# One operation per product term, and transposes planned with an advance, in a two-layer decoder trunk

## The chip, the cores and the metric

The kernel runs on one core of a Trainium2 chip. The metric is the time of one execution in microseconds (us), as the median of several runs. The engines of the core work side by side, each through its own queue in order: TensorE (matrix products and transposes, PE in the profile), VectorE (DVE), ScalarE (ACT), GpSimd (POOL) and SyncE (SP), which issues the transfers from memory.

## The reference, cut to what matters

256 tokens of width 1024 pass two layers. Each has a mixer (block-sparse attention with 16 heads in layer 0, dilated attention with 12 heads in layer 1) and a squared-ReLU MLP of width 4096, each followed by a layer norm.

```python
def reference(x, moba_w_qkv, moba_w_o, dil_w_qkv, dil_w_o, mlp_w_in, mlp_w_out, ...):
    h = x
    for i in range(DEPTH):
        ...
        h = layer_norm(DEEPNORM_ALPHA * h + mix, ln_mix_g[i], ln_mix_b[i])
        h = layer_norm(DEEPNORM_ALPHA * h + sq_relu_mlp(h, mlp_w_in[i], mlp_w_out[i]),
                       ln_mlp_g[i], ln_mlp_b[i])
    return h
```

With 256 tokens the block-sparse attention has one block, so it is plain causal attention.

## The kernel before

**Split products.** Each float32 operand is split into a high part (rounded to the matrix engine's float32r) and a low part (the rest). A product is the sum of three terms: high by high, high by low and low by high. For a weight tile, `load_w` (line 323) loads 128x1024 numbers into `raw`, ScalarE rounds them into `whi` (line 309) and VectorE subtracts to get `wlo` (line 314). `raw` has 4 buffers, `whi` and `wlo` 10 each (`NSLOT`). For the activations, `xs[0]` and `xs[1]` hold the transposed input of the current layer, each for four of the eight k tiles (128 rows of the width), with the high and the low part side by side.

**Kinds of product.** `mm_wstat` (line 440) keeps a weight tile stationary and moves all 256 tokens: it serves the query and key projections. `mm_xstat` (line 466) keeps 128 tokens of `xs` stationary and moves weight columns. It serves the values of both layers and the first chunk of each MLP, for one half of the tokens at a time (`m` is 0 or 1). In both, one recorded operation holds the three terms of one k tile, and needs the high and low part of both operands. `mm_wstat_wide` (line 453) serves the other MLP chunks. `mm_rows` (line 481) makes the output projections. All sums of one accumulation go to one PSUM buffer, so each recorded product depends on the one before it there.

**The planner.** Nothing is issued at once. Each step is recorded with `op` (line 100): its engine, an estimated cost, what it reads and writes. `Plan.order` (line 131) then fixes the order of every engine's queue. A first pass walks the operations in recorded order and gives each TensorE operation a due time, its start in that pass. A backward pass gives every other operation the latest time at which it must start for what follows, and lowers a due time where a successor needs it. Then the plan is simulated: on each engine, among the operations that can start earliest, the one with the lowest due time is taken (VectorE may wait a little for a more urgent one). Loads keep their recorded order. At run time every engine works through its queue in the planned order, whatever the real durations are.

**Stages.** Layer 0's query, key and value projections, scores, softmax and weighting follow `ORDER0`: `qk` is a pair of projections with the rotation (`rotate`, line 511: three products on VectorE, lines 514 to 519, which show as L501, a sum on GpSimd, L503, then splits), `v` the values (`do_v`), `s` the scores and the softmax, `o` the weighting, whose transposed weights ScalarE copies out as `pt` (L595). Then `out_and_ln` (line 722) does the output projection and the layer norm. The last `ntail` input tiles (from `TAIL`, one entry for each of the four sub-layers) are done half by half, the others for both halves at once. The entry for layer 1's mixer is `TAIL[2]`, which has six tiles in all.

**Junctions.** In `out_and_ln` the first half's products come first, then its `ln_half` (line 668), then the second half's products, then `between()`, then the second half's `ln_half`. `between` is the head of the next sub-layer, which works on the first half alone: for the MLPs the first chunk's `half(0)` (line 771) with `relu_sq_tok` (ScalarE lines 749 and 750 into `hrt`, then transposes), after layer 0's MLP the values of layer 1 (`layer1_head`). `ln_half` ends with two groups of four transposes (`transposes`, line 582, shown as L587) of the normed tokens `tok`, and a split into `xs`. The last sub-layer has no `between`.

Of the kernel before, what the change touches and what calls it, by code (L numbers as in the profile page):

```python
# [26 lines left out]
BIG = 3.0e38  # L27
NCH = DFF // 512
NX = (1, 1)
TAIL = (5, 5, 5, 8)  # L30
NSLOT = 10
ADD_ENG = "POOL"
ORDER0 = (
# [43 lines left out]


class Op:
    __slots__ = ("n", "eng", "cost", "fn", "preds", "succs", "bufs", "due", "wait", "ready", "end", "xfer", "early")  # L80


class Plan:
# [13 lines left out]
        self.first.setdefault(tag, b)  # L97
        return b

    def op(self, eng, cost, fn, reads=(), writes=(), xfer=0.0, early=0.0):  # L100
        o = Op()
        o.n, o.eng, o.cost, o.fn, o.xfer = len(self.ops), eng, cost, fn, xfer
        o.early = early
        o.preds, o.succs, o.bufs = set(), [], set()
        for group, is_write in ((reads, False), (writes, True)):
            for item in group:
                b, key = item if isinstance(item, tuple) else (item, None)
                o.bufs.add(b)
                for k, st in b.state.items():
                    if key is None or k is None or k == key:  # L110
                        if st[0] is not None:
                            o.preds.add(st[0])
                        if is_write:
                            o.preds.update(st[1])
                st = b.state.setdefault(key, [None, []])
                if is_write:
                    if key is None:
                        b.state = {None: [o, []]}
                    else:
                        st[0], st[1] = o, []  # L120
                else:
                    st[1].append(o)
        o.preds.discard(o)
        for p in o.preds:
            p.succs.append(o)
        for b in o.bufs:
            b.left += 1
        self.ops.append(o)
        return o

    def order(self):
        clock = {e: BEGIN[e] for e in ("PE", "SP")}
        bus = 0.0
        for o in self.ops:
            t = max([clock.get(o.eng, 0.0)] + [p.end + latency(p, o) for p in o.preds])
            o.end = t + o.cost
            if o.eng in clock:
                clock[o.eng] = o.end
            if o.xfer:
                bus = o.end = max(t + FETCH, bus) + o.xfer  # L140
            o.due = t if o.eng == "PE" else None
        t = clock["PE"]
        for o in reversed(self.ops):
            for q in o.succs:
# [104 lines left out]
def tile_trunk(  # L249
# [188 lines left out]
        return [(xs[kt // 4], (part, kt, m)) for part in range(2) for m in ms]  # L438

    def mm_wstat(ps, w):  # L440
        for kt in range(KT):

            def go(kt=kt):
                c = slice(kt * P, (kt + 1) * P)
                a, b = (xs[kt // 4].t[:, kt % 4, part, :] for part in range(2))
                first, last = kt == 0, kt == KT - 1
                mm(ps.t[:, :S], w.hi.t[:, c], a, first, False)
                mm(ps.t[:, :S], w.hi.t[:, c], b, False, False)
                mm(ps.t[:, :S], w.lo.t[:, c], a, False, last)

            op("PE", 0.36, go, [(w.hi, 0), (w.lo, 0)] + xk(kt, (0, 1)), [ps])

    def mm_wstat_wide(ps, w):
        def go_hi(kt):
# [8 lines left out]
        for kt in range(KT):  # L463
            op("PE", 0.12, lambda kt=kt: go_lo(kt), [(w.lo, 0)] + xk(kt, (0, 1)), [ps])

    def mm_xstat(ps, ws, m, n):
        t = slice(m * P, (m + 1) * P)
        for kt in range(KT):
            per = 1024 // n
            w = ws[kt // per]  # L470

            def go(kt=kt, w=w):
                c = slice((kt % per) * n, (kt % per + 1) * n)
                a, b = (xs[kt // 4].t[:, kt % 4, part, t] for part in range(2))
                mm(ps.t[:, :n], a, w.hi.t[:, c], kt == 0, False)
                mm(ps.t[:, :n], a, w.lo.t[:, c], False, False)
                mm(ps.t[:, :n], b, w.hi.t[:, c], False, kt == KT - 1)

            op("PE", 3 * (n / 2400 + 0.0135), go, [(w.hi, 0), (w.lo, 0)] + xk(kt, (m,)), [ps])

    def mm_rows(pieces, item, m):
        (ahi, alo, j), w, pos, total = item
# [99 lines left out]
    def transposes(ps, pairs, r):  # L582
        ident = late["ident"]

        def go():
            for c, src in pairs:
                nc.tensor.transpose(ps.t[:, c : c + P], src(), ident.t)  # L587

        op("PE", 0.109 * len(pairs), go, list(r) + [ident], [ps])

    halves = (slice(0, P), slice(P, S))

# [72 lines left out]
    def act_tiles():  # L665
        return mk([P, 4, S], F32R, "ahi", 3), mk([P, 4, S], F32R, "alo", 3)

    def ln_half(pieces, m, gb, last):
        g, b = gb
        z = xtok[m]  # L670
        step = min(n for _, _, n in pieces)
# [18 lines left out]
        for n in range(2):  # L690
# [12 lines left out]
            if not last:  # L703
                ps = psum("tp")
                transposes(
                    ps, [(j * P, lambda k=n * 4 + j: z.t[:, k * P : (k + 1) * P]) for j in range(4)], [(z, n)]
                )
                t = slice(m * P, (m + 1) * P)
                keys = [(n * 4 + j, m) for j in range(4)]
# [12 lines left out]
    def out_and_ln(acc, items, ntail, gb, last, between):  # L722
# [4 lines left out]
        for m in range(2):  # L727
# [2 lines left out]
                    mm_rows([piece], item, m)  # L730
            if m == 1 and between:
                between()
            ln_half(acc[m], m, gb, last)

    def relu_sq_T(ps, ahi, alo, j):
        u = mk([P, S], F32, "ta", 5)
# [23 lines left out]
    class Mlp:  # L760
# [10 lines left out]
        def half(self, m):  # L771
            ps = [psum("tp") for _ in range(self.nx)]
            for c in range(self.nx):
                mm_xstat(ps[c], self.ws[c], m, 512)
            for c in range(self.nx):
                relu_sq_tok(ps[c], m, *self.chunks[c])

# [38 lines left out]
    def layer0(between):  # L816
# [3 lines left out]
        def do_v(n):  # L820
# [4 lines left out]
            V[n] = []  # L825
            for m in range(2):
                ps = psum("tp" if n == m == 0 else "acc")
                mm_xstat(ps, ws, m, 512)
                V[n].append(evac_v(ps, 512))

        def softmax(q, k):
# [63 lines left out]
    def v1(i, m):  # L895
# [191 lines left out]
```

## Time and profile before

| | us |
|---|---|
| median of 3 runs | 579.99 (579.93 to 580.3) |
| the profiled execution | 579.34 |
| its span, first to last instruction | 577.2 |
| TensorE busy | 562.7 |
| VectorE busy | 431.3 |
| ScalarE busy | 299.9 |
| GpSimd busy | 36.9 |

A row of the timeline has the start and the duration in us, the engine, the line of the code, the operation, output and inputs by the program's names, shapes, and a count. In brackets stands how long the engine was idle just before and which engine and line ended that. PE is TensorE with matrix products, PEld its loading of the stationary operand, which runs beside. A matrix product is pipelined, so its modelled duration (0.39 us for 512 columns) is longer than the distance to the next one. Helpers record most operations, so line 318 stands for every matrix product, 309 for every rounding on ScalarE and 314 for every subtraction on VectorE.

### The profile page before, as it was taken

The numbers are of one execution on the slowest core, as the hardware profiler recorded it, in microseconds if no ns is written. First come the engines' busy times: TensorE is split into PE (matmuls) and PEld (weight loads), VectorE is DVE, ScalarE is ACT, GpSimd is POOL, SyncE is SP. The second block draws the span as 40 slices with busy tenths as digits, with TensorE's granted clock in tenths as the row PEclk, the third lists the DMA queues.
The fourth block names the chain that finished last, engine by engine and source line by source line (L and its number), as shares of the span: only waits on it lengthen the run. The fifth ranks groups of instructions, "written<-read, shape, count | busy, mean of one in ns | idle before, by whom it ended". The sixth has DMA issues, their size and how long they took to land.

```text
span 577.2 us, 8665 instructions
## 1 busy us (share of the span) xinstructions
PE 562.7 (97%) x3234; PEld 486.2 (84%) x3234; DVE 431.3 (75%) x771; ACT 299.9 (52%) x501; POOL 36.9 (6%) x41
## 2 busy tenths in 40 slices
PE   9899999999999999999999999999999999999994
PEld 8789887778888888888887998877888888888884
DVE  6899888998875675675678699988976756756544
ACT  6585666747554555454534445744754544544400
POOL 0210131010000000000000222000000000000000
PEclk9999999999999999999999999999999999999998
DMA  8646843728877666565525424544888655655101
GB/s 322 219 148 188 292 140 99 223 83 276 274 248 279 204 196 190 178 213 184 182 75 177 186 75 127 168 148 161 281 279 258 202 185 178 204 183 183 36 1 73
DMA packets 30281, 105.61 MB, mean 183 GB/s; under 512 B 3488, under 2 KB 4256, under 8 KB 30240
## 3 DMA queue, kind: packets, MB, share of 16 engines
q1 hardware_dynamic: 30240, 105.07, 55.6%
q8 instruction: 25, 0.41, 0.3%
q14 instruction: 16, 0.13, 0.1%
HBM read 104.01 MB, written 1.05 MB: 182 GB/s over the span
## 4 chain that ended last, share of the span: by engine, by line
PE 89%; DVE 7%; ACT 2%; issue 2%; POOL 1%; DVEq 0%; POOLq 0%
PE acc L318 50%; PE tp L318 37%; PE tp L587 2%; DVE wlo L314 2%; DVE ta L501 2%; DVE tok L508 1%; POOL ta L503 1%; ACT sc L573 1%; DVE klo L508 0%; DVE sc L580 0%; DVE xs L314 0%; DVE bst L682 0%; ACT hrt L749 0%; DVE qlo L314 0%; ACT hrt L750 0%
## 5 line engine op out<-in xcount | busy, mean ns | idle before, releaser
L314 DVE TENSOR_TENSOR wlo<-raw,whi 128x1024 fp32r<-128x1024 f32 (+2 forms) x185 | 225.7, 1226 | 88.1 <-ACT whi L309 86.7
L309 ACT ACTIVATE whi<-raw 128x1024 fp32r<-128x1024 f32 (+2 forms) x184 | 191.1, 1047 | 144.3 <-PE tp L318 64.9
L318 PE MATMUL acc<-whi,ahi 128*128 128x512 f32 (+1 forms) x312 | 119.5, 383 | 0.0
L318 PE MATMUL acc<-wlo,ahi 128*128 128x512 f32 (+1 forms) x312 | 117.5, 380 | 0.0
L318 PE MATMUL tp<-xs,whi 128*128 128x512 f32 x448 | 112.0, 392 | 0.0
L318 PE MATMUL acc<-whi,alo 128*128 128x512 f32 (+1 forms) x312 | 100.5, 380 | 0.0
L318 PEld LDWEIGHTS tp<-xs,whi 128*128 128x128 f32 x448 | 81.2, 189 | 14.7
L318 PE MATMUL acc<-xs,whi 128*128 128x256 f32 x448 | 83.6, 289 | 0.0
L318 PEld LDWEIGHTS acc<-xs,whi 128*128 128x128 f32 x448 | 70.4, 194 | 2.5 <-issue 1.6
L318 PEld LDWEIGHTS acc<-whi,ahi 128*128 128x128 f32 x312 | 58.8, 188 | 11.3 <-issue 0.9
L318 PEld LDWEIGHTS acc<-wlo,ahi 128*128 128x128 f32 x312 | 58.8, 188 | 10.4
L318 PEld LDWEIGHTS acc<-whi,alo 128*128 128x128 f32 x312 | 57.1, 189 | 10.4
L318 PEld LDWEIGHTS tp<-xs,wlo 128*128 128x128 f32 x448 | 61.0, 191 | 4.2
L318 PE MATMUL tp<-xs,wlo 128*128 128x256 f32 x448 | 62.7, 283 | 0.0
L318 PE MATMUL acc<-xs,wlo 128*128 128x256 f32 x224 | 62.1, 284 | 0.0
L318 PEld LDWEIGHTS acc<-xs,wlo 128*128 128x128 f32 x224 | 42.8, 192 | 0.0
L501 DVE TENSOR_TENSOR ta<-acc,ropet 64x256 f32<-64x256 f32 (+1 forms) x84 | 35.1, 421 | 9.7 <-PE acc L318 8.6
L309 ACT ACTIVATE ahi<-ta 128x256 fp32r<-128x256 f32 x56 | 22.9, 409 | 28.5 <-DVE ta L508 28.5
L503 POOL TENSOR_TENSOR ta<-ta,ta 128x256 f32<-128x256 f32 x28 | 28.2, 1014 | 119.8 <-DVE ta L501 105.8
L688 POOL TENSOR_TENSOR rstd<-rstd,expo 128x1 f32<-128x1 f32 x8 | 7.9, 987 | 414.6 <-DVE rstd L686 414.6
L318 PE MATMUL acc<-whi,xs 128*128 128x512 f32 (+1 forms) x112 | 32.9, 364 | 0.9 <-DVE xs L314 0.6
L501 DVE TENSOR_TENSOR ta<-tp,ta 128x256 f32<-128x256 f32 x56 | 23.5, 419 | 7.9 <-ACT ta L739 7.9
(83 smaller groups left out, 548.2 us busy)
## 6 DMA issues: line engine op xcount, KB each, us to landing
raw<-in_win_dram SPq DMA_DIRECT2D x64, 512.0 KB, 4.3
raw<-in_wout_dram SPq DMA_DIRECT2D x64, 512.0 KB, 4.2
raw<-in_wqk_dram SPq DMA_DIRECT2D x24, 512.0 KB, 4.0
raw<-in_wo_dram SPq DMA_DIRECT2D x14, 512.0 KB, 3.3
raw<-in_wv_dram SPq DMA_DIRECT2D x8, 512.0 KB, 6.1
g<-in_lng_dram SPq DMA_DIRECT2D x4, 512.0 KB, 7.0
b<-in_lnb_dram SPq DMA_DIRECT2D x4, 512.0 KB, 8.0
raw<-in_wv1a_dram SPq DMA_DIRECT2D x4, 512.0 KB, 3.2
```

The lines of the kernel that those rows point to most:

```text
L309: op("ACT", act(n, sbuf=sbuf), lambda: nc.scalar.activation(hi(), src(), AF.Copy), r, whi)
L314: lambda: nc.vector.tensor_tensor(lo(), src(), f32(hi()), op=ALU.subtract), list(r) + list(whi), wlo,
L318: nc.tensor.matmul(out_ap, lhsT, rhs, start=start, stop=stop)
L501: op("DVE", dve(n) + extra, lambda: nc.vector.tensor_tensor(out_ap(), a(), b(), op=alu), r, w)
L503: op("POOL", n / 480 + 0.17, lambda: nc.gpsimd.tensor_tensor(out_ap(), a(), b(), op=alu), r, w)
L508: lambda: nc.vector.scalar_tensor_tensor(dst(), a(), s(), b(), op0=o0, op1=o1), r, w,
L573: lambda: nc.scalar.activation(e(), e(), AF.Exp, bias=bias(), scale=-1.0, accum_out=total()), r, w,
L587: nc.tensor.transpose(ps.t[:, c : c + P], src(), ident.t)
L688: op("POOL", 0.98, lambda: nc.gpsimd.tensor_tensor(rs.t[:, 1:2], rs.t[:, 0:1], expo.t, op=ALU.pow), [(rs, 0), expo], [(rs, 1)])
```

## The change

`mm_wstat` records two operations for each k tile: first all high parts of the weights (two terms each), then all low parts. `mm_xstat` does the same and takes a word that says which operand lands late: for the MLP heads and layer 1's values it is `x`, so the terms with the high part of `xs` come first and the low part of `xs` last; for layer 0's values it is `w`, so the low part of the weights comes last. Operations depend only on the parts that they read. The number of matrix products and their shapes stay.

Operations can be recorded with `ahead`, which is taken off the due time. The transposes of the second half's layer norm have 1.5 us of it where there is a `between`. `TAIL[2]` goes from 5 to 6, so that all six tiles of layer 1's output projection are done half by half.

```diff
-TAIL = (5, 5, 5, 8)
+TAIL = (5, 5, 6, 8)
...
-    def op(self, eng, cost, fn, reads=(), writes=(), xfer=0.0, early=0.0):
+    def op(self, eng, cost, fn, reads=(), writes=(), xfer=0.0, early=0.0, ahead=0.0):
...
-        o.early = early
+        o.early, o.ahead = early, ahead
...
-            o.due = t if o.eng == "PE" else None
+            o.due = t - o.ahead if o.eng == "PE" else None
...
     def mm_wstat(ps, w):
+        def go_hi(kt):
+            for part in range(2):
+                mm(ps.t[:, :S], w.hi.t[:, kt * P : (kt + 1) * P], xs[kt // 4].t[:, kt % 4, part, :], kt + part == 0, False)
+
+        def go_lo(kt):
+            mm(ps.t[:, :S], w.lo.t[:, kt * P : (kt + 1) * P], xs[kt // 4].t[:, kt % 4, 0, :], False, kt == KT - 1)
+
         for kt in range(KT):
-
-            def go(kt=kt):
-                c = slice(kt * P, (kt + 1) * P)
-                a, b = (xs[kt // 4].t[:, kt % 4, part, :] for part in range(2))
-                first, last = kt == 0, kt == KT - 1
-                mm(ps.t[:, :S], w.hi.t[:, c], a, first, False)
-                mm(ps.t[:, :S], w.hi.t[:, c], b, False, False)
-                mm(ps.t[:, :S], w.lo.t[:, c], a, False, last)
-
-            op("PE", 0.36, go, [(w.hi, 0), (w.lo, 0)] + xk(kt, (0, 1)), [ps])
+            op("PE", 0.24, lambda kt=kt: go_hi(kt), [(w.hi, 0)] + xk(kt, (0, 1)), [ps])
+        for kt in range(KT):
+            op("PE", 0.12, lambda kt=kt: go_lo(kt), [(w.lo, 0)] + xk(kt, (0, 1)), [ps])
...
-    def mm_xstat(ps, ws, m, n):
+    def mm_xstat(ps, ws, m, n, late):
+
         t = slice(m * P, (m + 1) * P)
-        for kt in range(KT):
-            per = 1024 // n
+        per = 1024 // n
+
+        def go(kt, terms, first, last):
             w = ws[kt // per]
-
-            def go(kt=kt, w=w):
-                c = slice((kt % per) * n, (kt % per + 1) * n)
-                a, b = (xs[kt // 4].t[:, kt % 4, part, t] for part in range(2))
-                mm(ps.t[:, :n], a, w.hi.t[:, c], kt == 0, False)
-                mm(ps.t[:, :n], a, w.lo.t[:, c], False, False)
-                mm(ps.t[:, :n], b, w.hi.t[:, c], False, kt == KT - 1)
-
-            op("PE", 3 * (n / 2400 + 0.0135), go, [(w.hi, 0), (w.lo, 0)] + xk(kt, (m,)), [ps])
+            c = slice((kt % per) * n, (kt % per + 1) * n)
+            for i, (x_part, w_part) in enumerate(terms):
+                mm(
+                    ps.t[:, :n], xs[kt // 4].t[:, kt % 4, x_part, t], (w.hi, w.lo)[w_part].t[:, c],
+                    first and kt + i == 0, last and kt == KT - 1,
+                )
+
+        third = (1, 0) if late == "x" else (0, 1)
+        for terms, first, last in ((((0, 0), third[::-1]), True, False), ((third,), False, True)):
+            for kt in range(KT):
+                w = ws[kt // per]
+                op(
+                    "PE", len(terms) * (n / 2400 + 0.0135),
+                    lambda kt=kt, terms=terms, first=first, last=last: go(kt, terms, first, last),
+                    [((w.hi, w.lo)[i], 0) for i in {t[1] for t in terms}]
+                    + [(xs[kt // 4], (i, kt, m)) for i in {t[0] for t in terms}],
+                    [ps],
+                )
...
-        op("PE", 0.109 * len(pairs), go, list(r) + [ident], [ps])
+        op("PE", 0.109 * len(pairs), go, list(r) + [ident], [ps], ahead=ahead)
...
-            ln_half(acc[m], m, gb, last)
+            ln_half(acc[m], m, gb, last, 1.5 if m == 1 and between else 0.0)
...
-                mm_xstat(ps[c], self.ws[c], m, 512)
+                mm_xstat(ps[c], self.ws[c], m, 512, "x")
...
-                mm_xstat(ps, ws, m, 512)
+                mm_xstat(ps, ws, m, 512, "w")
...
-        mm_xstat(ps, wv[i], m, v_cols[i])
+        mm_xstat(ps, wv[i], m, v_cols[i], "x")
```

More of the change, by code (lines that the diff above doesn't have):

```diff
@@ L79 @@
 class Op:
-    __slots__ = ("n", "eng", "cost", "fn", "preds", "succs", "bufs", "due", "wait", "ready", "end", "xfer", "early")
+    __slots__ = ("n", "eng", "cost", "fn", "preds", "succs", "bufs", "due", "wait", "ready", "end", "xfer", "early", "ahead")
 class Plan:
@@ L580, in scale_by, with transposes @@
         op("DVE", dve(n, 1, True), lambda: nc.vector.tensor_scalar(e(), e(), s(), None, op0=ALU.mult), r, w)
-    def transposes(ps, pairs, r):
+    def transposes(ps, pairs, r, ahead=0.0):
         ident = late["ident"]
@@ L666, in act_tiles, with ln_half @@
         return mk([P, 4, S], F32R, "ahi", 3), mk([P, 4, S], F32R, "alo", 3)
-    def ln_half(pieces, m, gb, last):
+    def ln_half(pieces, m, gb, last, ahead):
         g, b = gb
@@ L705, in ln_half @@
                 transposes(
-                    ps, [(j * P, lambda k=n * 4 + j: z.t[:, k * P : (k + 1) * P]) for j in range(4)], [(z, n)]
+                    ps, [(j * P, lambda k=n * 4 + j: z.t[:, k * P : (k + 1) * P]) for j in range(4)], [(z, n)],
+                    ahead,
                 )
```

## The prediction

> **What bounds the kernel now.** I read the page first, then who waited for whom on TensorE, then the chain that ended last, and only then the instructions around each wait in order of time.
>
> ```profile
> span 577.2 us, 8665 instructions
> PE 562.7 (97%) x3234; PEld 486.2 (84%) x3234; DVE 431.3 (75%) x771; ACT 299.9 (52%) x501; POOL 36.9 (6%) x41
> PE 89%; DVE 7%; ACT 2%; issue 2%; POOL 1%; DVEq 0%; POOLq 0%
> ```
>
> TensorE is the bound: busy for 97% of the span and 89% of the chain. The change adds and removes no matrix product, so it can win only time in which TensorE stands still. The view of TensorE's own waits says how much that is and whom it waits for (total, times, longest, in us):
>
> ```profile
> PE tp L318 <- DVE wlo L314: 1.6, 1, 1.6
> PE tp L587 <- ACT hrt L750: 1.5, 2, 0.8
> PE tp L587 <- ACT pt L595: 1.2, 1, 1.2
> PE acc L318 <- DVE xs L314: 0.6, 1, 0.6
> PE tp L318 <- ACT pt L595: 0.5, 1, 0.5
> PE acc L318 <- ACT xs L309: 0.3, 1, 0.3
> ```
>
> These sum to 5.7 us, 1% of the span. That is nearly the whole field. The start (three warming products, then the first stages by `Stage.mms`) and the end after the last product are not touched.
>
> To price products I take undisturbed stretches of the chain:
>
> ```profile
> 147.74 10.91 PE acc L318 x48
> 335.39 5.76 PE acc L318 x48
> ```
>
> One product with 512 moving columns takes 10.91 / 48 = 0.227 us, one with 256 takes 5.76 / 48 = 0.12 us.
>
> **The change part by part.**
>
> *Value products of layer 0, and weights-stationary projections.* The first wait stands here.
>
> ```profile
> 14.94 1.06 ACT L309 ACTIVATE whi<-raw 128x1024 fp32r<-128x1024 f32 x1 [0.22 <-DMA raw<-in_wv_dram]
> 16.08 1.32 DVE L501 TENSOR_TENSOR ta<-acc,ropet 128x256 f32<-128x256 f32 x3 [2.65 <-PE acc L318]
> 16.60 0.39 PE L318 MATMUL tp<-whi,xs 128*128 128x512 f32 x1
> 17.31 1.21 DVE L314 TENSOR_TENSOR wlo<-raw,whi 128x1024 fp32r<-128x1024 f32 x1
> 18.58 0.50 PE L318 MATMUL tp<-wlo,xs 128*128 128x512 f32 x1 [1.59 <-DVE wlo L314]
> ```
>
> TensorE does one product with the high part of the value weights at 16.60 and then needs the low part. VectorE makes it only at 17.31 to 18.52, behind the rotation of the first query tile. Start to start the loss is 18.58 - 16.60 - 0.227 = 1.75 us. After the change both products with `w.hi` run first for all eight k tiles, for both token halves 32 products, 7.3 us. The low parts are wanted only after that, and the wait at 18.58 must go. But the order of terms within one accumulation is fixed, since each product depends on the one before it. So the next late thing is the high part of the last weight tile, and it is ScalarE's:
>
> ```profile
> 21.31 0.91 ACT L529 ACTIVATE khi<-ta,hm 128x256 fp32r<-128x256 f32 x2 [4.07 <-POOL ta L503]
> 22.43 1.99 ACT L309 ACTIVATE whi<-raw 128x1024 fp32r<-128x1024 f32 x2
> ```
>
> ScalarE stood 4.07 us in its in-order queue for the rotation's sum on GpSimd and made the next high part at 22.43 to 23.5. With three tiles there, TensorE has 24 products, 5.45 us, from 16.60 to 22.05. If ScalarE's order and times stay, it then waits about 1.5 us, and only 1.75 - 1.5 = 0.25 us is won. If the later due time of the low parts lets VectorE do the rotations first (now they stand behind a 1.21 us subtraction), GpSimd's sum and ScalarE's queue come 1.2 us earlier, the last high part is there at 22.3, and nearly all of the 1.75 us is won. The stretch speaks for caution:
>
> ```profile
> 16.50:30.00 13.50, 11.85 (x52) 9.07 (x51) 13.12 (x21) 6.45 (x11) 4.35 (x4) 1.00 0.53 171
> 30.00:41.00 11.00, 10.51 (x84) 9.59 (x83) 10.70 (x34) 8.92 (x24) 1.29 (x2) 1.00 0.62 194
> ```
>
> The third busy time is VectorE's: 13.12 of 13.50 and 10.70 of 11.00 us. It is full, so a wait removed on TensorE tends to come back at the next thing VectorE makes. In favour stands that in `mm_wstat` too the low parts are now due 16 products (1.9 us) into each group, which lets VectorE run that much behind without being noticed. I take 1.0 us of 0.25 to 1.75. The 0.5 us wait for `pt` near 40 us lies in the same stretch; I take 0.2 of it.
>
> *The wait for `pt` at 86 us.*
>
> ```profile
> 82.42 1.23 DVE L314 TENSOR_TENSOR wlo<-raw,whi 128x1024 fp32r<-128x1024 f32 x1
> 82.53 1.70 POOL L503 TENSOR_TENSOR ta<-ta,ta 128x256 f32<-128x256 f32 x1 [3.95 <-DVE ta L501]
> 84.27 0.42 ACT L309 ACTIVATE qhi<-ta 128x256 fp32r<-128x256 f32 x1 [2.84 <-POOL ta L503]
> 85.54 0.58 ACT L595 ACTIVATE pt<-tp 128x512 f32<-128x512 f32 x1
> 86.17 0.33 PE L587 MATMUL tp<-ident,sc 128*128 128x128 f32 x1 [1.17 <-ACT pt L595]
> ```
>
> ```profile
> L503 POOL TENSOR_TENSOR ta<-ta,ta x28: 727/742/1776, 19.5 to 360.4; 128x256 f32<-128x256 f32 x28
> ```
>
> GpSimd's sum has a median of 0.742 us, but took 1.70 us beside VectorE's subtraction; ScalarE's queue waited for it, `pt` behind it, and TensorE for `pt`. Nothing in the change aims at this. Only the phase of the subtractions moves, so the coincidence may go or come back: 0.6 of 1.17 us, bounds -1.17 and 1.17.
>
> The Trainium skill, GPSIMD Engine Reference, section "Key points", says that GpSimd shares its SBUF interfaces with VectorE and contends with VectorE instructions that read two SBUF inputs. The row agrees (1.70 against 0.742 us beside `raw` minus `whi`, which are two such inputs). By that rule every sum that falls beside a subtraction is about 1 us late after the change as well; the rival on the slow side below is that rule at work.
>
> *Junctions: layer norm to the next layer's head, three places.* In each, TensorE finishes the head's products for the first token half, transposes the second half, and needs `xs` of it.
>
> ```profile
> 128.17 1.04 PE L587 MATMUL tp<-ident,tok 128*128 128x128 f32 x8
> 128.87 0.59 ACT L309 ACTIVATE xs<-tp 128x512 fp32r<-128x512 f32 x1
> 130.03 0.33 PE L587 MATMUL tp<-ident,hrt 128*128 128x128 f32 x1 [0.82 <-ACT hrt L750]
> ...
> 306.36 1.41 DVE L508 SCALAR_TENSOR_TENSOR tok<-tok,rstd,b 128x512 f32<-128x512 f32 x2
> 308.05 1.03 PE L587 MATMUL tp<-ident,tok 128*128 128x128 f32 x8
> 308.74 1.08 ACT L309 ACTIVATE xs<-tp 128x512 fp32r<-128x512 f32 x2
> 309.38 0.50 PE L318 MATMUL acc<-whi,xs 128*128 128x512 f32 x1 [0.30 <-ACT xs L309]
> 310.70 0.50 PE L318 MATMUL acc<-whi,xs 128*128 128x512 f32 x1 [0.58 <-DVE xs L314]
> ...
> 388.33 1.28 DVE L314 TENSOR_TENSOR xs<-tp,xs 128x512 fp32r<-128x512 f32 x2
> 388.54 0.39 PE L318 MATMUL tp<-wlo,xs 128*128 128x512 f32 x1
> 389.07 0.73 PE L318 MATMUL tp<-whi,xs 128*128 128x512 f32 x2
> 396.05 0.33 PE L587 MATMUL tp<-ident,hrt 128*128 128x128 f32 x1 [0.66 <-ACT hrt L750]
> ```
>
> First junction (MLP 0). The products that open the second half now need only the high part, which ScalarE has ready at 128.87 + 0.59 = 129.46. With about 0.15 us to TensorE (309.28 to 309.38 in the second junction is 0.1) they start near 129.6 instead of waiting for the `hrt` transposes at 130.03. Those come in between later without a wait. Gain 0.4. Does the advance of 1.5 us do more here? In the planner's first pass, in recorded order, the `hrt` transposes stand between the head's products and these transposes. They come some 1.8 us after the products' end (`relu`, `square` and the latencies of the planner's table) and take 0.44 us, so the due time is 2.2 us past the end. Less 1.5 that is still 0.7 us past it, and no product of the first half is displaced. Were it displaced, the whole 0.82 us would go. Bounds 0 and 0.82.
>
> Second junction (values of layer 1). No `hrt` here, so the planner's due time is the end of the head's products, and 1.5 us before it means up to six products (6 x 0.227 = 1.4 us) follow the transposes. VectorE finishes the first half row at about 307.07 (half of 1.41 past 306.36), so four transposes can start near 307.2, 0.85 us earlier than 308.05, and cover the 0.30 us. The 0.58 us wait is for the low part, which is now wanted 16 products, 3.6 us, later; it goes in any case. Start to start the two cost about 1.2 us; I take 1.1, bounds 0.6 and 1.2.
>
> Third junction (MLP 1). The wait before 389.07 costs 389.07 - 388.54 - 0.227 = 0.30 us and is VectorE being late with `xs` of the first half. `TAIL` 6 moves item 0's six products of the second half (6 x 0.227 = 1.4 us) behind the first half's end, so the first half's layer norm starts that much earlier and the 0.30 us goes. The `hrt` wait behaves as in the first junction: 0.4 of 0.66 plus a little. I take 0.8, bounds 0.3 and 1.2. What `TAIL` gives up is item 0's second-half products as filling before the last attention outputs. They are still free to be chosen there, since they depend on nothing new.
>
> Four extra held slots cost nothing that I can see: `TAIL` 6 holds six of ten weight slots and the MLP head four. The tile after them is wanted only behind the second half's 24 products (5.5 us).
>
> *Against it.* A finer grain lets the planner cut groups at more places and a tighter TensorE meets other late things. I charge 0.5 us, between 0 and one wait of the largest size left, 1.2.
>
> Sum: 1.0 + 0.2 + 0.6 + 0.4 + 1.1 + 0.8 - 0.5 = 3.6 us. The profiled execution took 579.34 us (577.2 of span and 2.1 around it), which becomes 575.7. The median of the runs lies 0.65 higher, 579.99, so the forecast for the median is **576.4 us**.
>
> **The rivals.**
>
> *The wait only moves.* In layer 0's attention VectorE is full and ScalarE's high part is late next, so all three items there (1.8 us) vanish, and the junctions remain: 2.3 - 0.5 = 1.8, giving 578.2. For it speaks VectorE's 13.12 of 13.50 us; against it the later due low parts.
>
> *GpSimd's sums collide more often.* Place: the sixteen rotations of layer 0 (16.5 to 95 us). A sum beside a subtraction is 1 us late, and ScalarE's queue passes up to 1.17 us on to TensorE. One of them does so now. Price 1.17 us for each new one. Three eat 3.5 us, about the gain, so slower begins at four or more; with five the time is 576.4 + 5.9 = 582.3. For it: low parts that are due later move the subtractions in among the rotations. Against: most long sums do no harm today.
>
> *The plan does not follow.* The order is fixed from the planner's durations. If its due times leave the order around the waits as it is, nothing but noise is left: 580.0.
>
> *All waits go.* 1.75 + 0.5 + 1.17 + 0.82 + 1.2 + 1.2 = 6.6, nothing new: 573.4.
>
> **How the numbers follow.** Forecast 0.55 (its own range 574.5 to 577.8), the wait only moves 0.17, collisions 0.13, plan does not follow 0.08, all waits go 0.07. No change is within 0.2%, 1.16 us, about what this measurement tells apart: 578.8 to 581.2. Faster takes the forecast, all waits, and 0.11 of the second case: 0.73. Same takes 0.05 of the second and 0.05 of the fourth: 0.10. Slower takes the collisions and what is left: 0.17. The range for 8 in 10 reaches from 573.6 (short of all waits gone) to 579.9, which leaves out the collisions and half of the unchanged plan.
>
> **What would show it.** In the profile after: no TensorE wait for `wlo` between 16 and 19 us, but perhaps one for `whi` near 22; runs of 16 high products ahead of 8 low ones; at the second junction the `ident,tok` transposes inside the head's products, and no wait for VectorE's `xs`; at the first and third the first products of the second half ahead of the `hrt` transposes. The prediction is wrong if TensorE's waits in 16 to 95 us sum to more than the 3.3 us of now, or if more of GpSimd's sums take 1.7 us instead of 0.742 and ScalarE waits for them.

## The result, and the profile after

The changed kernel takes 577.39 us (median of six runs, 576.79 to 577.73), the kernel before beside it 579.97 us (six runs, 579.86 to 580.3). The ratio is 0.9955, 95% interval 0.9942 to 0.9967: 2.6 us faster. The forecast was 576.4, 3.6 us faster.

The page of the changed kernel's profile (this execution took 577.73 us), and TensorE's own waits by what they waited for (total, times, longest):

```profile
span 576.0 us, 8655 instructions
PE 563.0 (98%) x3234; PEld 486.9 (85%) x3234; DVE 430.1 (75%) x771; ACT 300.5 (52%) x501; POOL 40.4 (7%) x41
PE 95%; DVE 1%; DMA 1%; ACT 1%; issue 0%; POOL 0%; SPq 0%; DVEq 0%
```

```profile
PE acc L318 <- DVE ta L512: 1.8, 1, 1.8
PE acc L318 <- ACT whi L309: 1.5, 1, 1.5
PE tp L318 <- DVE warm L402: 1.2, 1, 1.2
PE tp L318 <- ACT xs L309: 0.6, 2, 0.3
PE tp L318 <- DVE mx L574: 0.5, 1, 0.5
```

TensorE's share of the chain rose from 89% to 95%. The second and third wait lie before 12 us, at the start. Of the six waits of before, the ones for `wlo`, `hrt`, `pt` (twice) and VectorE's `xs` are gone. The first two lines and the last are new. A second profile of the same kernel (a0 below) has the 0.5 us wait for `pt` again, at 41 us, so its absence here is not the change's doing.

A list of waits leaves out products that are slow without a wait, so the comparisons below use TensorE's **loss**: for each two matrix products in a row the distance between their starts, less 0.227 us for 512 columns, 0.120 for 256 and 0.109 for a transpose, summed over a stretch of the trace. In us:

| stretch (us) | before | after | forecast of the gain | gain |
|---|---|---|---|---|
| layer 0's attention (12 to 120) | 6.15 | 5.68 | 1.8 (1.0 + 0.2 + 0.6) | 0.47 |
| first junction (120 to 140) | 1.07 | 0.65 | 0.4 | 0.42 |
| second junction (290 to 320) | 1.48 | 0.01 | 1.1 | 1.47 |
| layer 1's attention (320 to 375) | 0.33 | 0.85 | none | -0.52 |
| third junction (375 to 400) | 1.58 | 1.03 | 0.8 | 0.55 |

The 0.5 us that the prediction charged for the finer grain names no place and is in no row. The gains sum to 2.4 us, which agrees with the 2.6 of the medians. The start is left out: it lost between 3.2 and 5.0 us over the profiles of this study, by when the first transfers came, in kernels that begin alike.

**The value products of layer 0**, in order of time:

```profile
17.18 1.32 DVE L512 TENSOR_TENSOR ta<-acc,ropet 128x256 f32<-128x256 f32 x3 [3.13 <-PE acc L318]
17.70 1.09 PE L318 MATMUL tp<-whi,xs 128*128 128x512 f32 x4
18.42 1.21 DVE L314 TENSOR_TENSOR wlo<-raw,whi 128x1024 fp32r<-128x1024 f32 x1
19.67 0.86 DVE L512 TENSOR_TENSOR ta<-acc,ropet 64x256 f32<-64x256 f32 x2
20.58 0.73 PE L318 MATMUL acc<-whi,xs 128*128 128x512 f32 x2 [1.78 <-DVE ta L512]
```

Four products run without the low part, as planned. Next in TensorE's order are the second token half's products, and they need a PSUM buffer of the pool `acc`, and the only free one comes from the key tile that VectorE still rotates. VectorE does three of the rotation's products, a subtraction of 1.21 us that nobody needs yet, and only then the two that let the buffer go. The 1.59 us wait for `wlo` has become a 1.78 us wait for the rotation.

**The junctions**, in the same order as before:

```profile
129.52 0.59 ACT L309 ACTIVATE xs<-tp 128x512 fp32r<-128x512 f32 x1
130.16 0.50 PE L318 MATMUL tp<-whi,xs 128*128 128x512 f32 x1 [0.30 <-ACT xs L309]
...
306.65 0.85 PE L318 MATMUL acc<-whi,xs 128*128 128x512 f32 x3
307.34 1.04 PE L598 MATMUL tp<-ident,tok 128*128 128x128 f32 x8
308.14 1.41 PE L318 MATMUL acc<-whi,xs 128*128 128x512 f32 x5
...
382.52 0.69 DVE L519 SCALAR_TENSOR_TENSOR tok<-tok,acc 128x512 f32<-128x512 f32 x1 [0.62 <-PE acc L318]
385.61 1.41 DVE L519 SCALAR_TENSOR_TENSOR tok<-tok,rstd,b 128x512 f32<-128x512 f32 x2
386.50 1.29 PE L598 MATMUL tp<-ident,tok 128*128 128x128 f32 x8
...
393.39 1.03 PE L598 MATMUL tp<-ident,tok 128*128 128x128 f32 x8
394.73 0.50 PE L318 MATMUL tp<-whi,xs 128*128 128x512 f32 x1 [0.30 <-ACT xs L309]
395.76 0.60 PE L598 MATMUL tp<-ident,hrt 128*128 128x128 f32 x4
```

At the first and third the second half's head products start on the high part of `xs` after a wait of 0.30 us for ScalarE's rounding, and the `hrt` transposes come later without a wait. At the second the transposes stand among the first half's products, and nothing is waited for. At the third, the first half's own transposes are new trouble: the last output product of the first half ends at about 382.5 (VectorE's `tok` at 382.52 waits for it), the transposes follow at 386.50 and take 1.29 us instead of 1.03, because they catch up with VectorE's `tok` of 385.61 to 387.0.

### The profile page after: what moved, and what is told of

It is laid out like the page before. It is cut to its first block, busy times and chain, and to the rows that moved or that the text cites. A ratio compares the mean times of both kernels' runs of the same rounds, so it can differ in the third digit from the quotient of the medians.

```text
span 576.0 us, 8655 instructions
## 1 busy us (share of the span) xinstructions
PE 563.0 (98%) x3234; PEld 486.9 (85%) x3234; DVE 430.1 (75%) x771; ACT 300.5 (52%) x501; POOL 40.4 (7%) x41
## 3 DMA queue, kind: packets, MB, share of 16 engines
HBM read 104.01 MB, written 1.05 MB: 182 GB/s over the span
## 4 chain that ended last, share of the span: by engine, by line
PE 95%; DVE 1%; DMA 1%; ACT 1%; issue 0%; POOL 0%; SPq 0%; DVEq 0%
PE acc L318 55%; PE tp L318 38%; PE tp L598 2%; DMA raw<-in_xw_dram 1%; DVE ta L512 0%; DVE tok L519 0%; POOL ta L514 0%; ACT xs L309 0%; ACT hrt L761 0%; DVE wlo L314 0%; SPq L305 0%; ACT whi L309 0%; ACT khi L540 0%; DVE klo L519 0%; DVE bst L693 0%
## 5 line engine op out<-in xcount | busy, mean ns | idle before, releaser
L318 PE MATMUL acc<-xs,whi 128*128 128x256 f32 x448 | 64.9, 288 | 1.5 <-ACT whi L309 1.5
L318 PEld LDWEIGHTS acc<-xs,whi 128*128 128x128 f32 x448 | 58.6, 192 | 4.2 <-issue 1.8
L514 POOL TENSOR_TENSOR ta<-ta,ta 128x256 f32<-128x256 f32 x28 | 31.7, 1137 | 117.1 <-DVE ta L512 112.6
L318 PE MATMUL acc<-xs,wlo 128*128 128x256 f32 x224 | 34.7, 284 | 0.0
L751 ACT ACTIVATE ta<-tp 128x256 f32<-128x256 f32 x56 | 21.0, 375 | 20.3 <-PE tp L318 20.2
L318 PE MATMUL acc<-whi,xs 128*128 128x512 f32 (+1 forms) x112 | 29.5, 371 | 1.8 <-DVE ta L512 1.8
```

What stands on the lines that cost most here:

```text
L318: nc.tensor.matmul(out_ap, lhsT, rhs, start=start, stop=stop)
L514: op("POOL", n / 480 + 0.17, lambda: nc.gpsimd.tensor_tensor(out_ap(), a(), b(), op=alu), r, w)
L751: op("ACT", act(S), lambda: nc.scalar.activation(u.t, ps.t[:, S:], AF.Copy), [ps], [u])
```

## The experiments

Twelve runs, each timed in five rounds beside the kernel before. The table has the ratio to before with its 95% interval, the median, and the losses of the five stretches above in the profiled run.

| kernel | ratio | us | layer 0 | 1st | 2nd | layer 1 | 3rd |
|---|---|---|---|---|---|---|---|
| before | 1 | 579.7 to 580.2 | 6.15 | 1.07 | 1.48 | 0.33 | 1.58 |
| e1 projections alone | 1.0004 [0.9994, 1.0014] | 580.36 | 6.73 | 1.10 | 1.40 | 0.51 | 1.28 |
| e2 layer 0's values alone | 1.0005 [0.9997, 1.0014] | 580.67 | 5.79 | 1.82 | 1.41 | 0.60 | 1.28 |
| e3 heads alone | 0.9978 [0.9968, 0.9988] | 578.8 | 6.18 | 0.62 | 0.58 | 0.56 | 1.55 |
| e4 advance alone | 0.9982 [0.9973, 0.9991] | 579.06 | 6.17 | 1.06 | 0.42 | 0.32 | 1.54 |
| h1 heads and advance | 0.9973 [0.9963, 0.9983] | 578.08 | 6.16 | 0.62 | 0.04 | 0.28 | 1.83 |
| the changed kernel again | 0.9957 [0.9943, 0.9971] | 577.42 | 5.53 | 0.63 | 0.04 | 0.86 | 1.03 |
| f1 changed, values as before | 0.9978 [0.9969, 0.9987] | 578.5 | 6.75 | 0.65 | 0.01 | 0.80 | 1.04 |
| f2 changed, another PSUM buffer | 0.9978 [0.9966, 0.999] | 578.85 | 7.82 | 0.64 | 0.01 | 0.81 | 1.08 |
| f3 changed, advance 3.0 | 0.9991 [0.9983, 1.0] | 579.59 | 5.54 | 0.57 | 0.02 | 2.49 | 1.42 |
| f4 changed, `TAIL` 5 | 0.9935 [0.9923, 0.9948] | 575.93 | 5.56 | 0.66 | 0.05 | 0.05 | 0.63 |
| d1 changed, `wlo` twice | 1.0009 [1.0001, 1.0018] | 580.09 | 9.27 | 0.64 | 0.03 | 0.84 | 1.05 |
| p1 changed, two `wlo` on GpSimd | 0.9917 [0.9904, 0.9931] | 575.09 | 3.62 | 0.64 | 0.08 | 0.33 | 1.41 |

### One part at a time, on the kernel before

e1 has only the new `mm_wstat`. e2 and e3 have the new `mm_xstat` for some calls, and `mm_xstat_old`, the old one, for the rest:

```diff
 e2
-                mm_xstat(ps, ws, m, 512)
+                mm_xstat(ps, ws, m, 512, "w")
 e3
-                mm_xstat(ps[c], self.ws[c], m, 512)
+                mm_xstat(ps[c], self.ws[c], m, 512, "x")
...
-        mm_xstat(ps, wv[i], m, v_cols[i])
+        mm_xstat(ps, wv[i], m, v_cols[i], "x")
```

> The kernel before with the new query and key projections alone (high parts of the weights first). Theory A (the gain comes place by place, and in layer 0's attention from the projections): the waits for `pt` at 40 and 86 us go, 1.0 to 1.7 us less, 578.3 to 579.0; the wait for `wlo` of 1.6 us at 18.6 us and the junctions stay as before. Rival B (the order is shuffled anew and every part alone moves the time by chance): no change beyond 0.5 us, or slower.

> The kernel before with layer 0's value products alone in the new order (low part of the weights last). Theory A (the wait only moves to the PSUM buffer that a rotation holds): the wait for `wlo` at 18.6 us is gone and one of 1.5 to 2 us for the rotation stands near 19 to 20 us; time within 0.5 us of before. Rival (the prediction's step: 1.0 us won): 579.0.

> The kernel before with the new order of terms in the MLP heads and layer 1's values alone (low part of xs last), no advance, tail 5. Theory A: at the second junction the wait for VectorE's xs (0.58) goes and the 0.30 for ScalarE's stays; at the first and third the second half starts 0.4 us earlier each, ahead of the `hrt` transposes; 1.4 to 1.7 us less, 578.3 to 578.6. Rival (the advance does it): under 0.5 us less.

e1 gained nothing, as its rival B had it. Its 1.6 us wait for `wlo` stayed, and one for VectorE's `mx` came at 88.6:

```profile
PE tp L587 <- DVE mx L563: 1.8, 2, 1.5
PE tp L318 <- DVE wlo L314: 1.6, 1, 1.6
```

e2 gained nothing either: layer 0's loss fell by 0.36 us, the first junction's rose by 0.75. Its `wlo` wait was gone and the wait for the rotation stood there (1.8 us). Why the first junction, 90 us later, lost more was not followed. e3 gained 1.3 us, at the first junction 0.45 and at the second 0.90. At the third, for which the prediction booked 0.4 for this order, it gained nothing (1.58 to 1.55): the wait for `hrt` shrank to 0.2 us, and one of 0.6 us for the second half's `tok` stood there instead.

e4 has the advance alone, h1 the advance and e3's order together:

```diff
-            o.due = t if o.eng == "PE" else None
+            o.due = t - o.ahead if o.eng == "PE" else None
...
-            ln_half(acc[m], m, gb, last)
+            ln_half(acc[m], m, gb, last, 1.5 if m == 1 and between else 0.0)
```

> The kernel before with the advance of 1.5 us alone. Theory A (it displaces products only at the second junction, where no `hrt` transposes stand in between): the first four transposes there come about 0.9 us earlier, the 0.30 us wait for ScalarE's xs goes, the 0.58 for VectorE's may stay; first and third junction as before; 0.3 to 0.6 us less, 579.4 to 579.7. Rival (it moves the transposes everywhere): 1.5 us less or more.

> The kernel before with the products' order in the MLP heads and layer 1's values and the advance of 1.5 together, and nothing else of the change (attention of layer 0 and TAIL as before). Theory A (junction gains add where they do not share a wait; both edits remove the same 1 us at the second junction): losses of about 0.65, 0.1 and 1.6 us at the three junctions against 1.08, 1.52 and 1.52 before, a gain of 1.6 to 1.9 us, 578.1 to 578.4, and the rest of the change (layer 0's attention and TAIL) is worth 0.7 to 1.0 us on top of it. Theory B (the junctions carry the whole gain): 577.3 to 577.6.

e4 gained 1.0 to 1.1 us, more than the 0.3 to 0.6 that was expected. The advance acts at the second junction alone (1.48 to 0.42). At the first and third the loss is as before, as the prediction had it: 1.5 us is short of displacing a product there. Together the two edits take the second junction to 0.04. h1's 1.66 us (579.74 less 578.08) is what the junctions are worth without the rest, within what was expected of adding gains.

### One part undone or moved, on the changed kernel

f1 records layer 0's values the old way; f2 gives both token halves of the first value group a buffer of the pool `tp`, which the rotation does not hold:

```diff
 f1
-                mm_xstat(ps, ws, m, 512, "w")
+                mm_xstat_old(ps, ws, m, 512)
 f2
-                ps = psum("tp" if n == m == 0 else "acc")
+                ps = psum("tp" if n == 0 else "acc")
```

> The changed kernel again, beside the next ones on one chip: 2.6 us under the kernel before, 0.5 either way. Its waits from the start of the values to 110 us the same as in the first profile; the first 10 us may differ with the transfers.

> The changed kernel, but layer 0's values recorded in the old way (three terms in one operation). Theory C (until about 90 us the chain runs through VectorE and ScalarE, and TensorE's waits there only change places): the 1.6 us wait for `wlo` is back, other waits up to 110 us are shorter, and the time is that of the changed kernel within 0.4 us. Rival D (the prediction: the new order of the values wins 1.0 us): 1.0 us slower than the changed kernel. Rival E (the new order costs, through the wait for the rotation and the lower granted clock behind it): 1 to 2 us faster.

> The changed kernel, with layer 0's first values for both token halves in `tp` buffers, so that the second half waits for no rotation. Theory C: the wait for the rotation (1.8 us) is gone, one of 1.0 to 1.5 us for ScalarE's high part of the last weight tile takes its place, and the time is that of the changed kernel within 0.4 us. Rival E (that wait sets the time): 1.5 to 2 us faster than the changed kernel.

f1 is 1.1 us slower than the changed kernel on the same chip (578.5 against 577.42, with ranges that overlap: 577.91 to 579.86 and 577.06 to 578.31): in the whole change the new order of the values is worth about that, though alone (e2) it gave nothing. But it is not won at the values. There f1 loses 1.76 us by the wait for `wlo`, and the changed kernel 1.95 by the wait for the rotation. What f1 has and the changed kernel has not is a wait near 87 us. Rows of f1, then of the changed kernel:

```profile
84.89 0.42 DVE L314 TENSOR_TENSOR qlo<-ta,qhi 128x256 fp32r<-128x256 f32 x1 [1.08 <-ACT qhi L309]
85.23 1.29 DVE L527 TENSOR_TENSOR ta<-acc,ropet 128x256 f32<-128x256 f32 x3
87.47 0.41 PE L613 MATMUL tp<-ident,sc 128*128 128x128 f32 x2 [1.55 <-DVE mx L589]
...
84.50 1.29 DVE L512 TENSOR_TENSOR ta<-acc,ropet 128x256 f32<-128x256 f32 x3 [0.32 <-PE acc L318]
86.52 0.44 DVE L314 TENSOR_TENSOR qlo<-ta,qhi 128x256 fp32r<-128x256 f32 x1
```

TensorE waits there for `mx`, which VectorE makes when it masks the scores for the softmax, right behind a rotation. In f1 the rotation stands behind a `qlo` that has to wait 1.08 us for ScalarE's `qhi`, and so it does in e1 and f2. In the changed kernel that `qlo` comes behind the rotation and two of the maskings, and nothing waits.

f2 took the wait for the rotation away and became 1.2 us (by the ratios) to 1.4 us slower, with a wide spread (577.79 to 581.12); theory C expected the same time. Its rows:

```profile
17.64 5.63 PE L318 MATMUL tp<-whi,xs 128*128 128x512 f32 x24
22.34 0.91 ACT L540 ACTIVATE khi<-ta,hm 128x256 fp32r<-128x256 f32 x2 [4.13 <-POOL ta L514]
23.47 1.99 ACT L309 ACTIVATE whi<-raw 128x1024 fp32r<-128x1024 f32 x2
24.56 1.20 PE L318 MATMUL tp<-whi,xs 128*128 128x512 f32 x4 [1.29 <-ACT whi L309]
```

This is the wait that the prediction named: 24 products in a row, then ScalarE's high part of the last tile, behind the rotation's sum. A wait removed returned at the next late thing. The 1.5 us wait for `mx` near 87 us is back too, and behind it TensorE ran slowly for a while (granted clock 0.68 from 88 to 92 us and 0.90 from 92 to 96, against 1.00 before), where f2 lost some 1.4 us more than f1 did.

f3 doubles the advance:

```diff
-            ln_half(acc[m], m, gb, last, 1.5 if m == 1 and between else 0.0)
+            ln_half(acc[m], m, gb, last, 3.0 if m == 1 and between else 0.0)
```

> The changed kernel with an advance of 3.0 us instead of 1.5. Theory A (the due time is 0.7 us past the head's products at the first and third junction, so 1.5 is too little there): both groups of transposes stand among the last products of the head, the two waits of 0.30 us for ScalarE's xs (0.47 us start to start) go, 0.7 to 0.9 us less than the changed kernel. Rival (the displaced products make `relu` and the `hrt` transposes late and give it back): 0.2 us or less.

f3 is 2.2 us slower than the changed kernel, against both expectations. At the first junction the transposes now stand earlier, and the loss fell by 0.06 us only. The price came elsewhere: layer 1's attention lost 2.49 us instead of 0.86 and the third junction 1.42 instead of 1.03. Three of its waits (0.7 us of the first and all of the second lie in layer 1's attention, the third at the third junction):

```profile
PE tp L318 <- ACT pt L606: 1.2, 2, 0.7
PE tp L318 <- ACT whi L309: 0.6, 1, 0.6
PE tp L318 <- DVE xs L314: 0.5, 1, 0.5
```

The edit touches no operation of layer 1's attention, so its plan changed with the due times elsewhere. GpSimd took 1.7 us for three of its sums between 335 and 365 us, but so it did in the changed kernel; what made these waits was not followed further.

f4 takes `TAIL[2]` back:

```diff
-TAIL = (5, 5, 6, 8)
+TAIL = (5, 5, 5, 8)
```

> The changed kernel with TAIL's third entry back at 5. Theory A (TAIL 6 gives: it freed the 0.30 us wait near 389, and the third junction lost 1.27 us with it against 1.52 before): the time rises by 0.3 to 0.8 us to about 577.9, and the wait for the low part of xs near 389 is back. Theory B (TAIL 6 takes: with it the second half's products of the first unit were spent as filler before the last attention outputs, only 18 products stand behind the first half's end instead of 24, and a wait of 0.5 us for VectorE's mx stands near 362): the time falls by 0.2 to 0.8 us to about 576.9, and TensorE's loss in 320 to 400 us sinks from 1.9 to below 1.5. Within 0.3 us both have about equal weight.

It is faster than the changed kernel by 1.2 us (0.9955 less 0.9935, of 580) to 1.5 us (575.93 against 577.42, with ranges that do not meet: 575.64 to 576.62 and 577.06 to 578.31). The theory that `TAIL` 6 takes time holds, and with more than the 0.2 to 0.8 that was expected of it; the wait for the low part of `xs` near 389, which `TAIL` 6 was to remove, did not come back either. 0.4 us of the difference lie at the third junction and 0.8 in layer 1's attention. The third junction of f4:

```profile
379.00 0.69 DVE L519 SCALAR_TENSOR_TENSOR tok<-tok,acc 128x512 f32<-128x512 f32 x1 [0.62 <-PE acc L318]
382.08 1.41 DVE L519 SCALAR_TENSOR_TENSOR tok<-tok,rstd,b 128x512 f32<-128x512 f32 x2
383.56 1.03 PE L598 MATMUL tp<-ident,tok 128*128 128x128 f32 x8
```

From VectorE's first-half `tok` at 379.00 to the transposes 4.6 us pass, filled by 21 products of the second half, and VectorE is done by 383.5. In the changed kernel it was 4.0 us (382.52 to 386.50) with 18 products, and none was left for the time behind the transposes; f4 has six there, before 385.8. `TAIL` 6 let the plan use second-half products as filling before the last attention outputs, so fewer were left where the first half's layer norm has to be covered.

The 0.8 us in layer 1's attention are of another kind. The changed kernel's rows:

```profile
358.66 1.70 POOL L514 TENSOR_TENSOR ta<-ta,ta 128x256 f32<-128x256 f32 x1 [1.26 <-DVE qlo L314]
360.39 0.91 ACT L540 ACTIVATE khi<-ta,hm 128x256 fp32r<-128x256 f32 x2 [1.50 <-POOL ta L514]
360.93 0.88 DVE L519 SCALAR_TENSOR_TENSOR klo<-ta,hm,khi 128x256 fp32r<-128x256 f32 x2 [0.84 <-ACT khi L540]
362.31 0.36 PE L318 MATMUL tp<-khi,qhi 128*128 128x256 f32 x1 [0.49 <-DVE mx L574]
```

and the same sum in f4:

```profile
357.88 0.73 POOL L514 TENSOR_TENSOR ta<-ta,ta 128x256 f32<-128x256 f32 x1 [1.40 <-DVE qlo L314]
```

The last sum takes 1.70 us in the one and 0.73 in the other, ScalarE and VectorE wait for it in turn, and TensorE 0.49 us at their end. That explains 0.65 of the 0.8 us; that `TAIL` 6 brings this collision about by more than a shift of the plan is not shown.

### Is layer 0's attention bound by VectorE?

In d1 `again` records the subtraction of a tile a second time, for four tiles. In p1 `lo_eng` gives two of the four subtractions to GpSimd:

```diff
 d1
-            ws = [load_w(wv0[n * 4 + j]) for j in range(4)]
+            ws = [load_w(wv0[n * 4 + j], again=n == 0) for j in range(4)]
 p1
+            ws = [load_w(wv0[n * 4 + j], lo_eng="POOL" if n == 0 and j in (0, 3) else "DVE") for j in range(4)]
```

> The changed kernel with the subtraction for the low part done twice for the four weight tiles of layer 0's first value group: 4 x 1.22 = 4.9 us more for VectorE between about 17 and 30 us, with the same values. Theory A (layer 0's attention is bound by VectorE, which has no idle time there): the time rises by 3 to 5 us, to 580.4 to 582.4, and TensorE's loss between 10 and 110 us grows from 5.6 to 9 or more. Theory B (TensorE bounds that stretch, and the waits are accidents of order): VectorE's slack later on takes up most of it, the time rises by 1 us at most, and the loss grows by less than 1.5.

> The changed kernel with the low parts of two of the four first value tiles (0 and 3) made by GpSimd instead of VectorE: 2.4 us less for VectorE. GpSimd took 0.74 us for a 128x256 sum, so about 3 us for such a tile, estimated by elements. Theory A (VectorE's work sets when the rotation releases its buffer, the 1.8 us wait near 20.6): the wait shrinks to below 1 us and the time falls by 0.5 to 1.5 us, to 575.9 to 576.9. Theory B (GpSimd's two subtractions stand before the rotation's sums in its queue, ScalarE's khi, qhi and whi are late behind them): the wait for VectorE is shorter, but one of 1 us or more for ScalarE's whi or pt takes its place, and the time is the same or up to 2 us slower.

d1 took 2.7 us (580.09 against 577.42) to 3.0 us (1.0009 less 0.9957, of 580) more than the changed kernel, at the lower end of the VectorE theory and far above the other, and layer 0's loss grew by 3.6 to 3.7 us. But this is no pure measure of VectorE's load. The plan moved the subtractions ahead of rotations, and behind two waits for `wlo` TensorE ran at half clock (the last two lines are windows of d1; the clock is the third number from the end):

```profile
PE tp L318 <- DVE wlo L336: 4.0, 2, 2.7
25.50:28.00 2.50, 2.15 (x4) 1.13 (x5) 2.46 (x5) 1.06 (x1) 0.11 (x1) 0.50 0.46 175
28.00:32.50 4.50, 4.50 (x12) 3.53 (x12) 4.30 (x11) 3.89 (x7) 2.44 (x4) 0.52 0.49 137
```

From 25.8 to 32.3 us the products lost 3.3 us that way. So d1 shows that more work of VectorE here reaches the end as lost time, and not how much of the loss is the work and how much the clock.

p1 took 2.3 us less than the changed kernel, more than the 0.5 to 1.5 that was expected: layer 0's loss fell by 1.9 to 2.1 us, that of layer 1's attention by 0.5, and the third junction's rose by 0.4. Its granted clock was 1.00 from 16.5 to 41 us. Its lines are one number higher:

```profile
14.93 2.42 POOL L315 TENSOR_TENSOR wlo<-raw,whi 128x1024 fp32r<-128x1024 f32 x1 [13.13 <-ACT whi L309]
16.75 2.96 DVE L513 TENSOR_TENSOR ta<-acc,ropet 128x256 f32<-128x256 f32 x7 [3.22 <-PE acc L319]
18.98 1.19 PE L319 MATMUL acc<-whi,xs 128*128 128x512 f32 x4 [0.62 <-DVE ta L513]
```

With the first subtraction on GpSimd, VectorE does the rotation's products in one go, the buffer comes free, and the wait shrinks from 1.78 to 0.62 us. No wait for `whi` took its place, since ScalarE gets the rotation's sum earlier too. p1 is the fastest kernel that was run; with `TAIL` 5 as well it might be faster still, which was not tried.

## Why the prediction came out as it did

The time fell on the forecast's side and in its range, 1.0 us above it. That it came so near is in part luck: layer 0 gave 1.3 us less than was booked, layer 1's attention lost 0.5 that nobody had forecast, the third junction gave 0.25 less, and against these stand 0.4 more at the second junction and the charge of 0.5. The field was also wider than the 5.7 us of waits that the prediction called nearly all of it: by loss the five stretches of before held 10.6 us. By its steps:

**Layer 0's values: the next late thing was another, and the place won nothing.** 1.0 us was booked. The step that failed is "the next late thing is the high part of the last weight tile, and it is ScalarE's". It counted 32 products on end, but the second token half needs a PSUM buffer, and that was still held by the rotation: 1.78 us, after four products. Start to start the place lost 1.76 us before and 1.95 after. ScalarE's wait stood behind it, 1.29 us in f2 where the prediction had 1.5. f1's 1.1 us agree with the 1.0 by luck: they come nearly 70 us later. That VectorE is full and the wait tends to come back there was in the prediction as a caution, and p1 bears it out.

**Layer 0 as a whole: mis-sized.** 1.8 us booked, 0.5 to 0.6 measured (6.15 to 5.68 and 5.53). The `pt` wait at 40 us (0.2 booked) is still there in the second profile. The wait at 86 us (0.6 booked) did go, 1.33 us start to start, and is the stretch's one clear gain. The prediction took it for a coincidence at which nothing in the change aims. But as a wait for `pt` or for `mx` it stands in all six kernels with the old order of the values (before, e1, e3, e4, h1, f1), and of the seven with the new order in f2 alone. So the new order removes it, from far off and by way of VectorE's queue; why the plan puts `qlo` elsewhere then was not followed. The rival "the wait only moves" describes this stretch better than the forecast's terms.

**First junction: right** (0.42 for 0.4), the way it was said: products on the high part, the advance idle.

**Second junction: under-sized.** 1.1 booked, with 1.2 as upper bound, and 1.47 measured. The bound was made from the two waits start to start (0.47 and 0.75 us); the second products behind them, which took 0.11 us longer than usual each, were left out. e4 shows that the transposes among the products take away most of the loss alone.

**Third junction: the step on `TAIL` ran the other way.** The prediction said that `TAIL` 6 moves six products behind the first half's end, and of the filling that this gives up before the last attention outputs only that those products "are still free to be chosen there". That freedom was the cost: they were chosen, and 18 were left instead of the 24 of before and the 27 of f4. It booked 0.8; the whole change got 0.55 here and lost 0.52 before it in layer 1's attention. With `TAIL` 5 the junction gains 0.95 and layer 1 another 0.28. Without this step the change would have stood at 575.9 (576.2 by f4's ratio), 0.2 to 0.5 us below the forecast.

**"A finer grain" was charged 0.5 us and seems to have paid instead.** f4 differs from h1 by the projections' and layer 0's values' order, and is 2.15 us faster on the same chip. Only 0.6 of the loss lies in layer 0; at the third junction it is 1.83 against 0.63, and in layer 1's attention 0.28 against 0.05. Of the two edits only the projections touch layer 1. That finer pieces fill those gaps better is read from this and was not tried by itself.

**The rival of the colliding sums was at work without winning.** Ten of GpSimd's 28 sums took about 1.7 us instead of seven, and all together 31.7 us (the first number behind the bar) instead of 28.2:

```profile
L514 POOL TENSOR_TENSOR ta<-ta,ta 128x256 f32<-128x256 f32 x28 | 31.7, 1137 | 117.1 <-DVE ta L512 112.6 <-ACT whi L309 3.2 <-DVE qlo L314 1.3
```

ScalarE waits for them somewhat longer too, so this sign of being wrong did come, while TensorE's waits in 16 to 95 us stayed below the 3.3 of before (1.8 and 2.8 in the two profiles). Three more at 1.17 us each would have cost 3.5 us; only one of the longer ones is seen to hold TensorE up, by 0.49 us at 362. f4 has nearly as many (30.8 us in all) and is faster: what counts is whether someone waits.

## What to carry to other kernels

When a wait in front of a full engine is taken away, look for the next thing that engine hands out, buffers included, and not only for the operand that comes after; taking work off that engine (p1) gave nearly as much as the whole change. Filling that a planner may use freely is used at the first gap, so whatever frees more of it early has to be counted as missing at the later one. Time the parts in combination: the order of layer 0's values was worth nothing alone and 1.1 us in the whole, and `TAIL` 6 cost a third of what the rest had won (1.2 to 1.5 of 3.8 us). And look where a gain arises, not only at its size: those 1.1 us were the booked ones by their size alone.

## What the hardware showed that was not expected

**Half clock after a short wait.** Windows of the changed kernel's trace (length; busy time and count for TensorE, its weight loads, VectorE, ScalarE, GpSimd; granted clock; DMA share; GB/s), then the same of the second run of that kernel:

```profile
22.00:25.50 3.50, 3.50 (x10) 2.68 (x10) 3.41 (x6) 3.09 (x5) 1.07 (x2) 0.51 0.69 206
```

```profile
22.00:25.50 3.50, 3.50 (x17) 2.87 (x17) 3.37 (x6) 2.41 (x5) 1.76 (x2) 1.00 0.70 261
```

In the first, eight products stood 0.427 us apart instead of 0.227, for 3.4 us, 1.5 us after the wait of 1.78 us. The second had the same wait and kept its clock. The Trainium skill, TensorE: Matmul & The Clock Gate, "What's actually happening" in Part 1, has the clock fall after at least one idle window of about 3.4 us. The length of the slow stretch agrees with that window, the idle time before it does not: the wait was about half as long. The 1.6 us that the slow products cost did not show: layer 0's loss was 5.68 us with them and 5.53 without. The second run has three places in their stead at which TensorE was held up by VectorE or ScalarE (`klo` at 32, `pt` at 41 and `mx` at 50 us, 1.5 us start to start in sum), and at full clock it met these. So in this stretch the slow products cost nothing that shows, since other engines set the pace.

**GpSimd slows VectorE as well.** In p1 the longest `klo` fell beside GpSimd's second subtraction (23.55 to 25.95):

```profile
L520 DVE SCALAR_TENSOR_TENSOR klo<-ta,hm,khi x28: 470/480/1719, 24.5 to 358.5; 128x256 fp32r<-128x256 f32 x28
```

It took 1.72 us against a median of 0.48. In the changed kernel the longest of the 28 took 0.96. The Trainium skill, GPSIMD Engine Reference, "Key points", names the shared interfaces and the contention with VectorE instructions that read two inputs from SBUF; this run puts the loss at up to 1.2 us on VectorE's side.
